# First norm of a decoder trunk: token tiles of chunk one loaded ahead of x's third chunk, squares after the scaling, first weights in two halves, another order of passes

## The chip, the core and the metric

The kernel runs on one core of one Trainium2 chip. The metric is the device time of one execution in microseconds (us), the median of several runs. TensorE is PE in the profile (its weight loads are PEld), VectorE is DVE, ScalarE is ACT, GpSimd is POOL and SyncE is SP. ACTq, SPq and POOLq are the engines' own instruction queues where they issue DMAs.

## The reference

Two layers over 16 meta tokens and 1024 tokens of width 1024. The change lies in the first norm and in the first input projections of layer 0.

```python
def rms_norm(x, gain):
    xf = x.astype(jnp.float32)
    y = xf * lax.rsqrt(jnp.mean(xf * xf, axis=-1, keepdims=True) + EPS)
    return (y * gain.astype(jnp.float32)).astype(x.dtype)

def conv_mixer(h, w_in, dw_kernel, dw_bias, ln_gain, ln_bias, w_out):
    proj = jnp.einsum("bld,dc->blc", h, w_in)
    u, g, z = jnp.split(proj, 3, axis=-1)
    v = u * jax.nn.sigmoid(g)
    # depthwise causal convolution of 31 taps over v, layer norm, SiLU,
    # times silu(z), projection with w_out
    ...

h = jnp.concatenate([meta, x], axis=1)          # 1040 tokens
for i in range(DEPTH):                          # layer 0: conv, layer 1: differential attention
    h = h + mixer_i(rms_norm(h, norm_gain[i]))
return rms_norm(h, final_norm_gain)[:, N_META:]
```

## The kernel before

Activations lie with the channels on the partitions: `x_t[k]` (k = 0 to 7) holds 128 channels by 1040 tokens. The tokens come in three chunks (`CH`) of 348, 346 and 346; numbers in names count from 0, so the first chunk is chunk 0. Weights come in strips of 128 output channels (`wf`, 512 KB). Each fp32 operand is split in two: a high part made by a copy on ACT (`wh` of the weights, `hh` of the activations) and a low part made by a subtraction (`wl`, `hl`; the function `lo_part`). `hh[k]` and `hl[k]` are the two halves of a tile that the profile calls hp. A projection of a strip on a chunk is 24 matmuls: 8 of wh with hh, 8 of wh with hl, 8 of wl with hh (`passes`, called by `project`).

The first norm runs in parts. The string `ORDER` sets in which order the code of these parts is written, each with its chunk number:

- u (`unscaled`): `hh` on ACT and `hl` on DVE are made from x times the gain, without the norm's scale, so that the strips g0 and u0 can be projected before the scale is known (p, `first_strips`). What is missing is multiplied into the result later (`sig0`, `vr0`).
- k (`load_tokens`): SP loads `chn` and `sub_g` and the nine tiles xk0 to xk8 (the last is called hsum), which hold 128 or 96 tokens on the partitions and their 1024 channels along the row. xk0 to xk2 are chunk 0, and so on.
- t (`statistics`): the sum of squares of each token, by a square with an accumulator on ACT (two tiles of a chunk) or a reduction on DVE (one tile); then the reciprocal root on a few numbers (`tk`); then diagonal matrices `dg` on DVE, which PE multiplies with ones (tile n0), so that the scale of each token stands on all partitions. ACT copies it to `n0_r`.
- s (`scaled`): DVE multiplies x by gain and scale in place, ACT copies it to `hh`, and DVE (k even) or POOL (k odd) makes `hl`. From these all other strips are projected, strip 1 (g1, u1) first.

After this the convolution stage runs strip by strip: ACT scales shifted copies (pr), POOL adds them (pb, L522), DVE does other taps (L535), PE projects the next strips (g, u, z).

The code's order is only the start: a scheduler orders each engine's instructions when the kernel is built, and each engine then runs its list strictly in that order. `tc.high_priority` moves instructions forward in it, `tc.issue_after(i)` puts one behind the instruction i. An SP DMA also waits for an earlier DMA whose semaphore it uses again, so that a limited number is under way. Weight strips have two buffers (`wf`); strips 0 and 1 of the list are g0 and u0, whose `wl` is made on POOL.

Of the kernel before, what the change touches and what calls it, by code (L numbers as in the profile page):

```python
# [15 lines left out]
ALU = mybir.AluOpType  # L16
# [46 lines left out]
DIR1 = True  # L63
WL = "GG"
SP_R = 2000
ORDER = "u0_p0_u1_p1_u2_k0_p2_t0_s0_t1_s1_t2_s2"
FC = [(512, 256), (768, 256)]
HXM = 6
WB = 2
# [23 lines left out]
def trunk(  # L93
# [63 lines left out]
    class Weights:  # L157
# [6 lines left out]
        def prepare(self):  # L164
            if self.done == len(self.order):
                return
            n = self.done
            src, eng = self.order[n]
            self.done += 1
            wf = gp.tile([P, KD, P], F32, tag="wf", name=f"wf{n}", bufs=2)  # L170
            SP.dma_start(out=wf, in_=src)
            keep = self.kept.get(n - len(self.order))
            if keep:
                wh, wl = keep()
            elif n in self.staged:
                wh, wl = stage(0, f"wh{n}", F32R), scratch[-1].tile([P, T], F32R, tag="vr", name=f"wl{n}", bufs=VR)
                wh, wl = [t[:, :D].rearrange("p (k c) -> p k c", c=P) for t in (wh, wl)]
            else:
                wh = gp.tile([P, KD, P], F32R, tag="wh", name=f"wh{n}", bufs=WB)
                wl = gp.tile([P, KD, P], F32R, tag="wl", name=f"wl{n}", bufs=WB)  # L180
            A.activation(out=wh, in_=wf, func=AF.Copy)  # L181
            lo_part(eng, wl, wf, wh.bitcast(F32))
            self.ready.append((wh, wl))

# [112 lines left out]
    with ExitStack() as st0:  # L297
# [40 lines left out]
        V.memset(tk, 1.0)  # L338
        x_sum = pair("n0")
        last_pair = pair("gu0")  # L340
        scale_of = {}

        def load(ci):
            c0, w = CH[ci]
# [4 lines left out]
        def statistics(ci):  # L349
# [5 lines left out]
            for b in range(9)[bs]:  # L355
                r0, n = TB[b]
                t = x_k[b][:n]
                if TKE.split("_")[ci][b % 3] == "A":
                    A.activation(out=t, in_=t, func=AF.Square, accum_out=tk[:n, 0, b : b + 1])
                else:  # L360
                    V.tensor_tensor_reduce(
                        out=t, in0=t, in1=t, scale=1.0, scalar=0.0, op0=ALU.mult, op1=ALU.add,
                        accum_out=tk[:n, 0, b : b + 1],
                    )
            with tc.high_priority(offset=SP_R):
                s, x, t, r = (tk[:, j, bs] for j in range(4))
                V.tensor_scalar(out=x, in0=s, scalar1=1.0 / D, scalar2=EPS, op0=ALU.mult, op1=ALU.add)
# [25 lines left out]
        def scaled(ci):  # L393
            c0, w = CH[ci]
            cs = slice(c0, c0 + w)
            for k in range(KD):
                t = x_t[k][:, cs]
                V.scalar_tensor_tensor(
                    out=t, in0=t, scalar=mod[:, k, 0:1], in1=scale_of[ci], op0=ALU.mult, op1=ALU.mult
                )  # L400
                A.activation(out=hh[k][:, cs], in_=t, func=AF.Copy)  # L401
                lo_part(V if k in LOV[ci] else G, hl[k][:, cs], t, hh[k][:, cs].bitcast(F32))

        def load_tokens(_):
            SP.dma_start(out=chn, in_=chan)
            SP.dma_start(out=sub_g, in_=subln)
            for (r0, n), t in zip(TB, x_k):
                SP.dma_start(out=t[:n], in_=xk[r0 : r0 + n])

        def first_strips(ci):  # L410
            for n, (kind, w_) in enumerate((("g", gw), ("u", uw))):
                o = last_pair[:, 512 * n : 512 * n + 512] if ci == 2 else mm(f"{kind}0_{ci}")
                (gates0, ups0)[n].extend(project(w_, hh, hl, lambda _: o, CH[ci : ci + 1]))

        gates0, ups0 = [], []
        SP.dma_start(out=mod, in_=model)
# [1 line left out]
        load(0)  # L418
        weights.prepare()
        load(1)  # L420
        load(2)
        gw, uw = weights.get(), weights.get()
        parts = {"u": unscaled, "p": first_strips, "t": statistics, "s": scaled, "k": load_tokens}
        for step in ORDER.split("_"):
            e = parts[step[0]](int(step[1]))
            if step == "t2":
# [885 lines left out]
```

## Time and profile before

| | us |
|---|---|
| median of 3 runs | 1464.42 (1463.52 to 1465.74) |
| the profiled execution, its own time | 1462.38 |
| its span, first to last instruction | 1460.6 |
| PE busy | 1411.1 (97%) |
| DVE busy | 1123.2 (77%) |
| ACT busy | 885.0 (61%) |
| POOL busy | 803.1 (55%) |

The shares are averages over stages. Up to about 73 us the first norm and strips 0 and 1 run; to about 530 us the convolution, in which POOL, DVE and PE are all nearly full; then the rest of layer 0 and the attention, in which PE is. A row of a timeline gives the start, the time from the first to the last of the instructions merged in it, what they are, and in brackets how long the engine was idle before and what ended that.

### The profile page before, as it was taken

How to read it: one execution, taken by the hardware profiler on the slowest of the kernel's cores; microseconds unless marked ns; L12 is line 12 of the kernel's file. 1: busy time of each engine (PE TensorE's matmuls, PEld its weight loads, DVE VectorE, ACT ScalarE, POOL GpSimd, SP SyncE). 2: the span in 40 equal slices, each digit the busy share in tenths (PEclk: the TensorE clock that was granted, in tenths of full speed). 3: DMA queues.
4: the chain of work that ended last, by engine and by line, in shares of the span. 5: the costliest groups of instructions: out<-in, count | busy, mean ns of one | idle time of the engine just before them, and what ended most of it. 6: DMA issues, size and time to landing. Idle time of an engine off the chain costs nothing.

```text
span 1460.6 us, 24069 instructions
## 1 busy us (share of the span) xinstructions
PE 1411.1 (97%) x8798; PEld 1323.8 (91%) x8798; DVE 1123.2 (77%) x2121; ACT 885.0 (61%) x1604; POOL 803.1 (55%) x640
## 2 busy tenths in 40 slices
PE   8899999999999999899999999999999999999997
PEld 7799999999999999899998878988889899897786
DVE  5999999999999998988545311578788687786774
ACT  5765655565556668766224411668778777786652
POOL 1599999999999940044014501525345354353572
PEclk9999999999999999999999999999999999999999
DMA  9121112112111232654544634223221322338532
GB/s 300 31 73 44 59 53 64 45 44 66 66 44 44 92 116 97 192 167 153 169 158 132 200 99 124 64 70 104 85 81 63 114 81 77 104 89 296 171 124 94
DMA packets 81128, 155.15 MB, mean 106 GB/s; under 512 B 7121, under 2 KB 46546, under 8 KB 79986
## 3 DMA queue, kind: packets, MB, share of 16 engines
q1 hardware_dynamic: 67906, 131.01, 28.8%
q0 software_dynamic: 3824, 13.37, 2.9%
q10 hardware_dynamic: 9280, 9.23, 1.9%
q8 instruction: 69, 1.13, 0.3%
q14 instruction: 49, 0.40, 0.1%
HBM read 111.06 MB, written 34.01 MB: 99 GB/s over the span
## 4 chain that ended last, share of the span: by engine, by line
PE 51%; POOL 16%; DVE 13%; ACT 7%; issue 7%; DMA 5%; SPq 1%; POOLq 0%; DVEq 0%; ACTq 0%
POOL pb L522 15%; PE c L199 8%; PE v L199 6%; PE q L199 5%; PE k L199 5%; PE za L199 5%; PE z L199 4%; PE ao L199 3%; PE o L199 3%; ACT pr L521 2%; PE s L1000 2%; PE s L1001 2%; PE u L199 2%; PE tp L1034 2%; DVE wl L155 2%
## 5 line engine op out<-in xcount | busy, mean ns | idle before, releaser
L522 POOL TENSOR_TENSOR pb<-pr,pb 128x521 f32<-128x521 f32 (+1 forms) x272 | 386.6, 1430 | 14.7
L521 ACT ACTIVATE pr<-vr,chn 128x521 f32<-128x521 f32 x224 | 150.6, 724 | 129.7 <-POOL pb L522 129.5
L199 PE MATMUL c<-b,wh 128*128 128x260 f32 x1024 | 186.3, 284 | 3.7 <-ACT sz L447 1.6
L535 DVE SCALAR_TENSOR_TENSOR ev<-vr,chn,ev 128x520 f32<-128x520 f32 x240 | 181.1, 754 | 1.2
L181 ACT ACTIVATE wh<-wf 128x1024 fp32r<-128x1024 f32 x115 | 121.0, 1052 | 96.2 <-PE c L199 54.2
L199 PE MATMUL g<-hp,wh 128*128 128x346 f32 (+1 forms) x752 | 154.6, 329 | 13.5 <-ACT hp L401 5.3
L199 PEld LDWEIGHTS c<-b,wh 128*128 128x128 f32 x1024 | 158.8, 189 | 4.6 <-ACT sz L447 1.9
L199 PE MATMUL u<-hp,wh 128*128 128x346 f32 (+1 forms) x752 | 158.0, 323 | 2.3 <-ACT wh L181 2.2
L155 DVE TENSOR_TENSOR wl<-wf,wh 128x1024 fp32r<-128x1024 f32 x81 | 128.7, 1591 | 39.8 <-ACT wh L181 39.1
L199 PE MATMUL c<-b,wl 128*128 128x260 f32 x512 | 144.4, 284 | 3.5 <-DVE wl L155 3.5
L199 PEld LDWEIGHTS g<-hp,wh 128*128 128x128 f32 x752 | 126.8, 191 | 18.2 <-ACT hp L401 5.5
L155 POOL TENSOR_TENSOR wl<-wf,wh 128x1024 fp32r<-128x1024 f32 x34 | 84.7, 2490 | 97.8 <-ACT wh L181 54.1
L199 PE MATMUL z<-hp,wh 128*128 128x346 f32 (+1 forms) x768 | 134.9, 321 | 0.8 <-ACT sig L479 0.8
L535 DVE SCALAR_TENSOR_TENSOR od<-xs,wc,od 128x520 f32<-128x520 f32 x176 | 132.5, 753 | 0.0
L199 PEld LDWEIGHTS u<-hp,wh 128*128 128x128 f32 x752 | 126.8, 189 | 3.2 <-ACT wh L181 3.2
L707 POOL TENSOR_TENSOR total<-hsq,total 128x520 f32<-128x520 f32 x12 | 20.5, 1710 | 194.4 <-DMA wf<-conv_out 98.1
L199 PEld LDWEIGHTS z<-hp,wh 128*128 128x128 f32 x768 | 124.1, 188 | 1.2 <-ACT sig L479 1.1
L1008 ACT ACTIVATE p<-p,st 128x272 f32<-128x272 f32 (+7 forms) x128 | 100.5, 785 | 39.8 <-DVE st L1003 39.3
L199 PEld LDWEIGHTS c<-b,wl 128*128 128x128 f32 x512 | 97.1, 190 | 4.1 <-DVE wl L155 4.0
L199 PE MATMUL g<-hp,wl 128*128 128x346 f32 (+1 forms) x376 | 83.6, 321 | 0.0
L199 PE MATMUL v<-wv,g 128*128 128x512 f32 x352 | 83.5, 394 | 0.0
L1000 PE MATMUL s<-k,q 128*128 128x256 f32 (+6 forms) x224 | 77.0, 348 | 5.3 <-DVE st L1003 5.3
(298 smaller groups left out, 3433.2 us busy)
## 6 DMA issues: line engine op xcount, KB each, us to landing
wf<-conv_in SPq DMA_DIRECT2D x48, 512.0 KB, 3.6
wf<-conv_out SPq DMA_DIRECT2D x32, 512.0 KB, 3.9
wf<-attn_in SPq DMA_DIRECT2D x32, 512.0 KB, 3.7
wf<-attn_out SPq DMA_DIRECT2D x17, 512.0 KB, 3.6
sz_d<-sz ACTq DMA_DIRECT2D x32, 260.0 KB, 3.7
szr<-sz_d SPq DMA_DIRECT2D x16, 520.0 KB, 4.5
v<-v_d POOLq DMA_DIRECT2D x8, 1024.0 KB, 5.3
ya_d<-yb SPq DMA_DIRECT2D x28, 256.0 KB, 2.5
```

What stands on the lines that cost most here:

```text
L155: return eng.tensor_tensor(out=out_, in0=full, in1=hi, op=ALU.subtract)
L181: A.activation(out=wh, in_=wf, func=AF.Copy)
L199: PE.matmul(o, a[k], b[k], start=start and i == 0, stop=stop and i == tot - 1)
L521: A.activation(out=d, in_=src, func=AF.Copy, scale=w)
L522: G.tensor_tensor(out=dst, in0=d, in1=dst, op=ALU.add)
L535: V.scalar_tensor_tensor(out=dst, in0=src, scalar=w, in1=dst, op0=ALU.mult, op1=ALU.add)
L707: (V if SQA[m] == "V" else G).tensor_tensor(out=total[:, ns], in0=sq, in1=total[:, ns], op=ALU.add)
L1000: PE.matmul(o[:, :wm], q2[m][:, qs], k2[m][:, c0 : c0 + wm], start=True, stop=False)
L1001: PE.matmul(o[:, :wm], q2[m][:, qs], kl2[m][:, c0 : c0 + wm], start=False, stop=True)
L1008: A.activation(out=p[:, :n], in_=p[:, :n], func=AF.Exp, scale=-1.0, bias=least, accum_out=st[:, 1:2],)
L1034: PE.transpose(tp[:, (kb - kb0) * P : (kb - kb0 + 1) * P], p0[:, kb * P : (kb + 1) * P], ident)
```

## The change

- `load_tokens` gets a chunk number and loads three tiles. xk0 to xk2 are issued ahead of x's chunk 2, xk3 to xk5 behind weight strips 2 and 3, then `chn` and `sub_g`, then xk6 to xk8.
- `ORDER` puts t0 ahead of u2 and p2, and s0 ahead of t1.
- In `statistics` the squares on ACT are put behind the last copy of `scaled` issued so far, the reductions on DVE behind the last multiplication of it.
- Weight strip 0 comes in two DMAs of 256 KB, one from SP and one from ACT, and its high part in two copies.
- `first_strips` writes the matmuls itself: for g0 on chunk 0 the hl matmuls follow two behind the hh ones; for all others the order is hh, wl, hl.

```diff
-ORDER = "u0_p0_u1_p1_u2_k0_p2_t0_s0_t1_s1_t2_s2"
+ORDER = "u0_p0_u1_p1_t0_u2_p2_s0_t1_s1_t2_s2"
...
             wf = gp.tile([P, KD, P], F32, tag="wf", name=f"wf{n}", bufs=2)
-            SP.dma_start(out=wf, in_=src)
+            if n:
+                SP.dma_start(out=wf, in_=src)
+            else:
+                for q, ks in ((SP, slice(0, KD // 2)), (A, slice(KD // 2, KD))):
+                    q.dma_start(out=wf[:, ks], in_=src[:, ks])
...
-            A.activation(out=wh, in_=wf, func=AF.Copy)
+            for ks in (slice(0, KD),) if n else (slice(0, KD // 2), slice(KD // 2, KD)):
+                A.activation(out=wh[:, ks], in_=wf[:, ks], func=AF.Copy)
...
-        scale_of = {}
+        scale_of, scaled_by, gained_by = {}, [], []
...
-                    A.activation(out=t, in_=t, func=AF.Square, accum_out=tk[:n, 0, b : b + 1])
+                    with tc.issue_after(scaled_by[-1]) if scaled_by else ExitStack():
+                        A.activation(out=t, in_=t, func=AF.Square, accum_out=tk[:n, 0, b : b + 1])
                 else:
-                    V.tensor_tensor_reduce(
+                    with tc.issue_after(gained_by[-1]) if gained_by else ExitStack():
+                        V.tensor_tensor_reduce(
...
-                V.scalar_tensor_tensor(
+                e = V.scalar_tensor_tensor(
                     out=t, in0=t, scalar=mod[:, k, 0:1], in1=scale_of[ci], op0=ALU.mult, op1=ALU.mult
                 )
-                A.activation(out=hh[k][:, cs], in_=t, func=AF.Copy)
+                gained_by.append(e.ins)
+                scaled_by.append(A.activation(out=hh[k][:, cs], in_=t, func=AF.Copy).ins)
...
-        def load_tokens(_):
-            SP.dma_start(out=chn, in_=chan)
-            SP.dma_start(out=sub_g, in_=subln)
-            for (r0, n), t in zip(TB, x_k):
+        def load_tokens(ci):
+            for (r0, n), t in list(zip(TB, x_k))[3 * ci : 3 * ci + 3]:
...
-                (gates0, ups0)[n].extend(project(w_, hh, hl, lambda _: o, CH[ci : ci + 1]))
+                c0, w = CH[ci]
+                cs = slice(c0, c0 + w)
+                wh, wl = w_
+                ab = [[(wh, hh, k) for k in range(KD)], [(wh, hl, k) for k in range(KD)], [(wl, hh, k) for k in range(KD)]]
+                if ci == 0 and n == 0:
+
+                    ab = [j for two in zip_longest(ab[0], [None] * 2 + ab[1]) for j in two if j] + ab[2]
+                else:
+                    ab = ab[0] + ab[2] + ab[1]
+                for j, (a, x, k) in enumerate(ab):
+                    PE.matmul(o[:, :w], a[:, k], x[k][:, cs], start=j == 0, stop=j == 3 * KD - 1)
+                (gates0, ups0)[n].append((c0, w, o[:, :w]))
...
         load(1)
+        load_tokens(0)
         load(2)
         gw, uw = weights.get(), weights.get()
-        parts = {"u": unscaled, "p": first_strips, "t": statistics, "s": scaled, "k": load_tokens}
+        load_tokens(1)
+        SP.dma_start(out=chn, in_=chan)
+        SP.dma_start(out=sub_g, in_=subln)
+        load_tokens(2)
+        parts = {"u": unscaled, "p": first_strips, "t": statistics, "s": scaled}
```

What the scheduler makes of it, at three places. The first is PE's list where the scale of chunk 1 (n0 from dg1) is spread over the partitions, during strip 1 on chunk 0 (g1_0 and u1_0 with weights 2 and 3); before:

```order
L199 MATMUL g1_0_621<-hp6_101,wh2_165 128x348
L199 MATMUL u1_0_646<-hp6_101,wh3_611 128x348
L376 MATMUL n0_124<-dg1_426,ones_63 128x128 x2
L199 MATMUL g1_0_621<-hp7_102,wh2_165 128x348
L199 MATMUL u1_0_646<-hp7_102,wh3_611 128x348
L376 MATMUL n0_124<-dg1_426,ones_63 128x96
L199 MATMUL g1_0_621<-hp0_95,wh2_165 128x348
```

and after:

```order
L204 MATMUL u1_0_648<-hp5_100,wl3_614 128x348
L204 MATMUL u1_0_648<-hp6_101,wl3_614 128x348
L204 MATMUL u1_0_648<-hp7_102,wl3_614 128x348
L383 MATMUL n0_124<-dg1_428,ones_63 128x128 x2
L383 MATMUL n0_124<-dg1_428,ones_63 128x96
L204 MATMUL g1_1_676<-hp0_95,wh2_170 128x346
L204 MATMUL u1_1_701<-hp0_95,wh3_613 128x346
```

The scale of chunk 1 stood after 14 of the 48 matmuls of strip 1 on chunk 0 and now stands behind all 48; that of chunk 2 (n0 from dg2), in the same way, after 12 of strip 1 on chunk 1 before and behind all 48 now, and that of chunk 0 behind all of chunk 2 of strips 0 before, and in the midst of it now.

The second is DVE's list around the scaling of chunk 0 (x0 to x7 times n0); before:

```order
L375 TENSOR_SCALAR dg0_385<-ident_65,tk_122 96x96
L361 ISA xk7_121,tk_122<-xk7_121 128x1024
L361 ISA tk_122 128x1
L155 TENSOR_TENSOR wl3_612<-wf3_609,wh3_611 128x1024
L233 TENSOR_TENSOR tk_122<-tk_122 128x3
L367 TENSOR_SCALAR tk_122<-tk_122 128x3
L234 SCALAR_TENSOR_TENSOR tk_122<-tk_122 128x3
L483 TENSOR_TENSOR sig0_506<-g0_0_185,n0_r_112 128x348
L485 TENSOR_TENSOR vr0_504<-u0_0_210,n0_r_112 128x348
L235 SCALAR_TENSOR_TENSOR tk_122<-tk_122 128x3
L398 SCALAR_TENSOR_TENSOR x0_87<-x0_87,mod_76,n0_124 128x348
```

and after, from the end of that scaling:

```order
L405 SCALAR_TENSOR_TENSOR x7_94<-x7_94,mod_76,n0_124 128x348
L368 ISA xk4_118,tk_122<-xk4_118 128x1024
L368 ISA tk_122 128x1
L155 TENSOR_TENSOR wl2_171<-wf2_168,wh2_170 128x1024
L476 TENSOR_SCALAR chn_86<-chn_86 128x16x31
L841 TENSOR_SCALAR sub_s_8266<-sub_g_77 128x1
L155 TENSOR_TENSOR hp0_95<-x0_87,hp0_95 128x348
L155 TENSOR_TENSOR hp2_97<-x2_89,hp2_97 128x348
L155 TENSOR_TENSOR hp4_99<-x4_91,hp4_99 128x348
L155 TENSOR_TENSOR wl3_614<-wf3_611,wh3_613 128x1024
L155 TENSOR_TENSOR hp6_101<-x6_93,hp6_101 128x348
```

The reductions of xk4 and xk7 and the low parts of weights 2 and 3 stood ahead of chunk 0's scaling; now xk4, both low parts and the work on `chn` stand behind it, between the scaling and chunk 0's hl, and xk7 in the same way behind chunk 1's scaling.

The third is ACT's list at the start, its DMAs and the copies of the first weight strip (wh0) and of chunk 0; before:

```order
L347 DMA x1_88<-xt 128x348
L347 DMA x3_90<-xt 128x348
L347 DMA x5_92<-xt 128x348
L181 ACTIVATE wh0_129<-wf0_127 128x1024
L347 DMA x7_94<-xt 128x348
L387 ACTIVATE hp0_95<-x0_87,mod_76 128x348
```

and after:

```order
L175 DMA wf0_127<-conv_in 128x512
L352 DMA x1_88<-xt 128x348
L352 DMA x3_90<-xt 128x348
L186 ACTIVATE wh0_130<-wf0_127 128x512 x2
L352 DMA x5_92<-xt 128x348
L352 DMA x7_94<-xt 128x348
L394 ACTIVATE hp0_95<-x0_87,mod_76 128x348
```

The second half of the weights goes out ahead of x1 and x3, and the DMA of x5 moves behind the copies that wait for these weights.

## Rows read from the trace of the kernel before

**Rows 1.** The page's part 4, shares of the chain that ended last.

```profile
PE 51%; POOL 16%; DVE 13%; ACT 7%; issue 7%; DMA 5%; SPq 1%; POOLq 0%; DVEq 0%; ACTq 0%
```

**Rows 2.** Stretches: length; busy us (instructions) by engine, PEclk, DMA share, GB/s.

```profile
0.00:17.10 17.10, 12.26 (x45) 9.95 (x46) 10.56 (x20) 13.03 (x24) 5.57 (x8) 1.00 0.91 311
...
40.00:47.00 7.00, 3.65 (x13) 3.65 (x14) 6.74 (x18) 6.26 (x15) 3.24 (x4) 0.52 0.22 75
...
73.00:530.00 457.00, 449.48 (x2819) 446.56 (x2818) 439.44 (x618) 272.48 (x421) 440.33 (x299) 1.00 0.19 60
530.00:580.00 50.00, 50.00 (x310) 49.49 (x309) 41.29 (x62) 34.78 (x53) 0.00 (x0) 1.00 0.30 92
```

**Rows 3.** Timeline of PE, first 75 us: start, us, what [idle before].

```profile
6.89 5.74 PE L199 MATMUL g<-hp,wh 128*128 128x348 f32 x14 [1.74 <-ACT hp L387]
14.31 0.92 PE L199 MATMUL g<-hp,wh 128*128 128x348 f32 x2 [1.67 <-DVE hp L388]
15.06 1.42 PE L199 MATMUL g<-hp,wl 128*128 128x348 f32 x8
...
34.09 1.44 PE L199 MATMUL gu<-hp,wl 128*128 128x346 f32 x8
...
43.35 0.66 PE L199 MATMUL g<-hp,wh 128*128 128x348 f32 x1 [5.31 <-ACT hp L401]
...
55.63 0.81 PE L376 MATMUL n<-dg,ones 128*128 128x128 f32 x6
...
69.67 1.44 PE L199 MATMUL u<-hp,wl 128*128 128x346 f32 x8
```

**Rows 4.** Timeline of POOL, first 75 us.

```profile
6.45 2.37 POOL L155 TENSOR_TENSOR wl<-wf,wh 128x1024 fp32r<-128x1024 f32 x1 [5.13 <-ACT wh L181]
11.36 2.51 POOL L155 TENSOR_TENSOR wl<-wf,wh 128x1024 fp32r<-128x1024 f32 x1 [2.55 <-ACT wh L181]
43.76 3.61 POOL L155 TENSOR_TENSOR hp<-x,hp 128x348 fp32r<-128x348 f32 x4 [29.89 <-ACT hp L401]
...
67.19 8.41 POOL L522 TENSOR_TENSOR pb<-pr,pb 128x521 f32<-128x521 f32 x5
```

**Rows 5.** Timeline of DVE around the two POOL operations of the start.

```profile
6.87 2.32 DVE L388 SCALAR_TENSOR_TENSOR hp<-x,mod,hp 128x348 fp32r<-128x348 f32 x1 [5.72 <-ACT hp L387]
...
11.57 2.68 DVE L388 SCALAR_TENSOR_TENSOR hp<-x,mod,hp 128x348 fp32r<-128x348 f32 x1
```

**Rows 6.** Timeline of DVE, 33 to 63 us.

```profile
33.56 1.22 DVE L361 CUSTOM_DVE_ANT_0 xk<-xk 128x1024 f32<-128x1024 f32 x1
...
34.78 1.22 DVE L155 TENSOR_TENSOR wl<-wf,wh 128x1024 fp32r<-128x1024 f32 x1
...
40.81 0.52 DVE L483 TENSOR_TENSOR sig<-g,n_r 128x348 f32<-128x348 f32 x1
...
48.48 1.37 DVE L155 TENSOR_TENSOR hp<-x,hp 128x348 fp32r<-128x348 f32 x3
...
51.46 3.96 DVE L398 SCALAR_TENSOR_TENSOR x<-x,mod,n 128x346 f32<-128x346 f32 x8
...
59.65 2.99 DVE L398 SCALAR_TENSOR_TENSOR x<-x,mod,n 128x346 f32<-128x346 f32 x6
```

**Rows 7.** Timeline of ACT, first 75 us.

```profile
5.31 1.06 ACT L181 ACTIVATE wh<-wf 128x1024 fp32r<-128x1024 f32 x1 [3.28 <-DMA wf<-conv_in]
...
6.27 3.91 ACT L387 ACTIVATE hp<-x,mod 128x348 fp32r<-128x348 f32 x8
...
56.48 0.46 ACT L378 ACTIVATE n_r<-n 128x346 f32<-128x346 f32 x1 [0.53 <-PE n L376]
...
65.81 2.58 ACT L521 ACTIVATE pr<-vr,chn 128x521 f32<-128x521 f32 x4
```

**Rows 8.** SP's own queue at the start: start, us of the issue.

```profile
1.20 0.43 SPq L171 DMA_DIRECT2D wf<-conv_in  x1
```

**Rows 9.** The page's part 6: DMA issues, KB each, us to landing.

```profile
ya_d<-yb SPq DMA_DIRECT2D x28, 256.0 KB, 2.5
```

More of the change, by code (lines that the diff above doesn't have):

```diff
@@ L358, in statistics @@
                 if TKE.split("_")[ci][b % 3] == "A":
-                    A.activation(out=t, in_=t, func=AF.Square, accum_out=tk[:n, 0, b : b + 1])
-                else:
-                    V.tensor_tensor_reduce(
-                        out=t, in0=t, in1=t, scale=1.0, scalar=0.0, op0=ALU.mult, op1=ALU.add,
-                        accum_out=tk[:n, 0, b : b + 1],
-                    )
+                    with tc.issue_after(scaled_by[-1]) if scaled_by else ExitStack():
+                        A.activation(out=t, in_=t, func=AF.Square, accum_out=tk[:n, 0, b : b + 1])
+                else:
+                    with tc.issue_after(gained_by[-1]) if gained_by else ExitStack():
+                        V.tensor_tensor_reduce(
+                            out=t, in0=t, in1=t, scale=1.0, scalar=0.0, op0=ALU.mult, op1=ALU.add,
+                            accum_out=tk[:n, 0, b : b + 1],
+                        )
             with tc.high_priority(offset=SP_R):
```

## The prediction

> **What bounds the kernel now.** I read first the chain that ended last: more than half of it is PE, then POOL and DVE [rows 1]. Then the stretches: from 73 to 530 us PE works 449.5 of 457 us, POOL 440.3 and DVE 439.4, and from 530 to 580 us PE works all of the time [rows 2]. So after the start three engines are full together: what the start saves stays saved if PE, POOL and DVE all get it, and what one of them loses is lost. The start itself is read from the timelines. PE waits 1.74 us for its first hh and 1.67 us for the last hl but one of chunk 0 [rows 3], then runs 128 matmuls from 15.06 to 35.53 us, 0.16 us each, and then has little to do until 43.35 us, with 5.31 us idle at the end, because the scaled chunk 0 is not there [rows 3]. DVE scales chunk 1 from 51.46 and chunk 2 from 59.65 us [rows 6], PE ends strip 1 at 71.1 us [rows 3], and POOL begins to add taps at 67.19 us [rows 4]. These last three are the marks at which the new start must be early.
>
> **The first weights.** The strip is issued at 1.20 us and its copy on ACT starts at 5.31 [rows 8, 7]. A DMA of 256 KB elsewhere lands in 2.5 us [rows 9], so the halves land between 3.7 us and no earlier than now; I take 4.2, since they and three x tiles share the engines: 1.1 us gained, bounds 0 and 1.6. The Trainium skill, "DMA: Bandwidth & Descriptors", section "Issuing engines are not separate DMA queues", says that DMAs of different issuing engines run on the same 16 DMA engines and that several issuers save only the time of issuing. By that the halves would be worth one issue, 0.4 us, and the forecast below would be 0.7 us later. No run here shows the halves yet.
>
> **Chunk 0 up to its last hl.** ACT then copies the weights until about 5.25, POOL starts wl0 at 5.35 and holds DVE's first hl until 8.05: before, POOL's operation ran from 6.45 to 8.82 and DVE's, started at 6.87, ended at 9.19 [rows 4, 5]. Seven more at 0.49 each (0.49 from the eight of 3.96 us [rows 6]) would put the start of the eighth at 10.95. ACT needs 3.91 us for its eight copies [rows 7] and 1.06 for the next weights, so POOL's wl1 starts at 10.3, or up to 0.5 us later if the x tiles whose DMA moved behind the copies, or the weights, are late. That is ahead of the eighth hl, which is held as one was before: started at 11.57, ended at 14.25, POOL from 11.36 for 2.51 us [rows 4, 5]. With POOL from 10.6 the last hl ends near 13.5, against 14.7 before: 1.2 us early.
>
> **Loading xk0 to xk2 earlier.** By 17.1 us the DMAs have moved 311 GB/s, 5.3 MB [rows 2]; that is the first two strips (1.0 MB), two chunks of x (2.8 MB) and these three tiles (1.4 MB). So they land at about 17 to 18 us. x's chunk 2 comes about 4 us later, near 22, and is needed by PE only at 26.5 (below): nothing is lost. The sums of squares of xk0 to xk2 and the few small steps behind them are ready by 25.
>
> **Scale of chunk 0.** In PE's new list 97 matmuls stand between the last hl of chunk 0 and the last two that spread this scale; 97 at 0.16 from 13.65, with the first of the three, is 29.4. From such matmuls to the first scaled tile it takes 0.85 us to ACT's copy (55.63 to 56.48), 0.46 for it, and about 0.45 each for the multiplications of g0 and u0 (0.52 with the start-up): 2.2 us, here 2.1 as one of the three is done [rows 3, 7, 6]. The scaling starts at 31.5; before, PE's first matmul with its result was at 43.35 [rows 3]. So about 10 us are won here, and the question is what is kept.
>
> **Strip 1 on chunk 0.** The scaling takes 3.9 us (35.4). Behind it DVE now has xk4 (1.22), wl2 (1.22) and 0.45 us of work on the taps before the first hl (0.43) [rows 6]: 38.7. These have two operands in SBUF, and POOL makes its four hl of 0.9 us each just then [rows 4]; each may hold DVE up, 0 to 1.4 us in all. I take 1.2, since POOL held the operations of rows 5 for its whole length: 40.0. Two hl, wl3 and the fourth hl follow (0.86, 1.14 and 0.43): 42.4. PE has ended strips 0 at 35.0 and the 16 hh matmuls at 37.6, so it idles 2.4 us, and after the fourth hl it still has 20 matmuls: 45.7.
>
> **Scale of chunks 1 and 2.** Both stand behind all 48 matmuls of the strip in PE's new list, though dg1 is ready at about 44. Chunk 1's scaling starts at 45.7 + 2.2 = 47.9, 3.6 us earlier than before (51.46). Then scaling 3.9, POOL's hold 0 to 0.9 (I take 0.5), xk7 1.22, first hl 0.43: 54.0. From here PE has 32 matmuls, 5.1 us: 59.1. Chunk 2's scaling starts at 59.1 + 2.2 = 61.3, while it was 59.65 [rows 6]. The 10 us have gone: before, DVE alone set the pace and the scales were spread in the middle of a strip; now DVE waits for PE behind each strip, and PE for DVE's hl. What follows is the same work in nearly the same order, so PE ends strip 1 near 72.8 instead of 71.1, and POOL starts at about 68.8, after ACT's first copies of 2.58 us for four [rows 7]: **1.6 us later**. The bounds: no hold by POOL and the best DMA time give 59.0 for chunk 2, full holds and no gain from the halves 63.3; so 0.7 us gained to 3.7 lost.
>
> **The other edits.** Putting wl ahead of hl lets PE run where hl is late; in strips 0 DVE's hl of chunks 1 and 2 are ahead of PE anyway, so it is worth nothing there. The interleaved hl of g0 saves the six hl matmuls that before ran behind hh, which lay in the wait for DVE: nothing. `chn` comes about 10 us later than before and is first needed at 39: nothing. SP's queue has as many DMAs as before, ACT's one more, issued while ACT has no work; the next strip's DMA waits for wl2 as before and is needed after 70 us: nothing.
>
> **Sum.** 1462.38 for the profiled execution + 1.6 = 1464.0; the median of the runs is 2.0 above the profiled one, so 1466.0, bounds 1463.7 to 1468.1.
>
> **Rivals.** (1) *The eighth hl gets ahead of wl1.* Its start (10.95) and that of wl1 (10.3 to 10.8, later if the moved x tiles land later) are close. If DVE starts first, the last hl ends at 11.45, and then dg0, ready at 24.5, holds PE's list instead: 2.0 us less, 1464.0. The Trainium skill, "SBUF — State Buffer", section "Who interferes with whom", has it that a DVE instruction with two SBUF inputs and a GpSimd one that reads SBUF exclude each other, and that the one issued first blocks the other fully. The two holds of rows 4 and 5, where POOL was first both times, agree with it; by that rule this rival hangs on which of the two starts first. Against it: 0.2 us or more are missing.
> (2) *The convolution is dealt better.* PE idles 7.5 us between 73 and 530 us [rows 2], and the scheduler has ordered this stretch anew on PE, ACT and DVE. If half of this idle time goes, or the waits between DVE and PE in strip 1 turn out half as long, some 5 us are gained on the forecast: 1461.0. For it: the new list has the work for the next strips ahead; against: POOL is 96% busy there (440.3 of 457), and its list has hardly changed.
> (3) *PE's clock falls in strip 1.* After the idle time up to 43.35 the granted clock was 0.52 over 40 to 47 us, the lower of the two levels (1.2 GHz), while two shorter waits within the first 17 us left it at 1.00 [rows 3, 2]. In the new list PE waits about 2 us for chunk 1's scaling, then works two matmuls per 0.49 us, then waits 1.7 us. If the clock falls there, 32 matmuls on the way to chunk 2's scale take 0.28 us (13 in 3.65 us of work over 40 to 47 [rows 2]) instead of 0.16: 3.8 us later, 1469.8, slower. It decides if PE is idle as long as before 43.35; the waits counted here are each half of that, which speaks against it.
> (4) *The start is as early as it is meant to be*, all three marks 4 us early, because DVE's work behind each scaling finds no hold and PE reaches the scales earlier than counted: 1460.4. It needs both other ends at once.
>
> **Numbers.** Forecast 0.45, rival 1 0.2, rival 2 0.13, rival 3 0.12, rival 4 0.1. A measurement of this kernel can tell 0.2%, 2.9 us, from no change. Faster by more: rivals 2 and 4 but for a small part, with a little of rival 1, 0.23. Slower by more: rival 3 and a third of the forecast's own range, 0.26. Within: 0.51. The predicted time is 1466.0. The range reaches into rivals 2 and 3: 1460.6 to 1469.6.
>
> **What would show it.** The weights' first copy at 4.2 us; the last hl of chunk 0 behind POOL's wl1; chunk 0's scaling at 31.5, chunk 1's at 47.9, chunk 2's at 61.3; PE's waits of 2 us ahead of the first hl of strip 1 and ahead of chunk 1; POOL's first tap near 68.8. If chunk 2's scaling starts before 58, the loop between PE and DVE is shorter than I say; if the marks are as forecast and the time is not, the cause is the convolution's new order.

## The result and the profile after

The kernel after takes 1473.22 us (median of 7 runs, 1469.20 to 1479.60) against 1464.06 beside it: ratio 1.0057, 95% interval 1.0044 to 1.0071. It is 8 to 9 us slower; 1466.0 was forecast, with a range that ended at 1469.6. The profiled execution took 1477.28 us, with a span of 1475.5. It is the second longest of its seven, and that of the kernel before (1462.38) is shorter than any of the seven beside it, so the two spans differ by more than the medians do.

The start, from the timeline of ACT (start, us, what, in brackets the idle time before and what ended it); it answers [rows 7]:

```profile
5.01 0.63 ACT L186 ACTIVATE wh<-wf 128x512 fp32r<-128x512 f32 x1 [2.98 <-DMA wf<-conv_in]
5.55 0.61 ACT L186 ACTIVATE wh<-wf 128x512 fp32r<-128x512 f32 x1
...
12.38 1.06 ACT L186 ACTIVATE wh<-wf 128x1024 fp32r<-128x1024 f32 x1 [1.64 <-DMA wf<-conv_in]
18.19 1.06 ACT L365 ACTIVATE xk<-xk 128x1024 f32<-128x1024 f32 x1 [0.94 <-DMA xk<-xk]
...
21.87 1.06 ACT L365 ACTIVATE xk<-xk 96x1024 f32<-96x1024 f32 x1 [2.52 <-DMA xk<-xk]
```

POOL, same columns, answering [rows 4]:

```profile
6.24 2.35 POOL L155 TENSOR_TENSOR wl<-wf,wh 128x1024 fp32r<-128x1024 f32 x1 [4.93 <-ACT wh L186]
13.52 2.40 POOL L155 TENSOR_TENSOR wl<-wf,wh 128x1024 fp32r<-128x1024 f32 x1 [4.93 <-ACT wh L186]
...
72.84 27.05 POOL L544 TENSOR_TENSOR pb<-pr,pb 128x521 f32<-128x521 f32 x18 [1.84 <-ACT pr L543]
```

DVE, answering [rows 5, 6]:

```profile
7.45 4.97 DVE L395 SCALAR_TENSOR_TENSOR hp<-x,mod,hp 128x348 fp32r<-128x348 f32 x8 [6.29 <-DMA x<-xt]
13.95 5.79 DVE L395 SCALAR_TENSOR_TENSOR hp<-x,mod,hp 128x346 fp32r<-128x346 f32 x8 [1.54 <-ACT hp L394]
...
38.42 1.73 DVE L368 CUSTOM_DVE_ANT_0 xk<-xk 128x1024 f32<-128x1024 f32 x1
40.09 2.01 DVE L155 TENSOR_TENSOR wl<-wf,wh 128x1024 fp32r<-128x1024 f32 x1
...
46.93 0.66 DVE L382 TENSOR_SCALAR dg<-ident,tk 128x128 f32<-128x128 f32 x3
50.94 3.97 DVE L405 SCALAR_TENSOR_TENSOR x<-x,mod,n 128x346 f32<-128x346 f32 x8
...
60.16 0.66 DVE L382 TENSOR_SCALAR dg<-ident,tk 128x128 f32<-128x128 f32 x3
65.09 2.99 DVE L405 SCALAR_TENSOR_TENSOR x<-x,mod,n 128x346 f32<-128x346 f32 x6
```

PE, answering [rows 3]:

```profile
7.46 5.43 PE L429 MATMUL g<-hp,wh 128*128 128x348 f32 x16 [2.34 <-ACT hp L394]
...
27.99 0.49 PE L383 MATMUL n<-dg,ones 128*128 128x128 f32 x2 [2.43 <-DVE dg L382]
...
42.97 0.59 PE L204 MATMUL g<-hp,wh 128*128 128x348 f32 x2 [1.83 <-DVE hp L155]
...
48.68 0.80 PE L383 MATMUL n<-dg,ones 128*128 128x128 f32 x6
52.08 0.42 PE L204 MATMUL g<-hp,wh 128*128 128x346 f32 x1 [2.60 <-ACT hp L409]
57.75 0.58 PE L204 MATMUL g<-hp,wh 128*128 128x346 f32 x2 [1.14 <-DVE hp L155]
...
62.90 0.80 PE L383 MATMUL n<-dg,ones 128*128 128x128 f32 x6
66.23 2.59 PE L204 MATMUL g<-hp,wh 128*128 128x346 f32 x5 [2.53 <-ACT hp L409]
...
76.39 1.44 PE L204 MATMUL u<-hp,wl 128*128 128x346 f32 x8
```

Read these together. dg1 stands on DVE at 47.6 us and PE reaches it at 48.68; dg2 stands at 60.8 and PE reaches it at 62.90, each time behind the whole strip: 1.1 and 2.1 us late. Then PE waits 2.60 and 2.53 us for the scaling that this scale releases, and in strip 1 on chunks 0 and 1 it waits 1.83 and 1.14 us for the first hl. That is the loop between PE and DVE of the prediction. POOL's first tap comes at 72.84 us; it was at 67.19 [rows 4].

Stretches of the same trace: length; busy us (instructions) of PE, PEld, DVE, ACT, POOL; PE's granted clock; DMA share; GB/s. The third and fourth answer [rows 2]:

```profile
52.00:56.00 4.00, 3.92 (x14) 3.62 (x15) 4.00 (x7) 4.00 (x9) 3.28 (x4) 0.59 0.01 4
66.00:73.00 7.00, 6.77 (x20) 5.57 (x21) 7.00 (x16) 5.17 (x11) 3.86 (x5) 0.53 0.00 0
73.00:530.00 457.00, 448.32 (x2806) 446.32 (x2805) 430.33 (x615) 275.05 (x424) 441.76 (x298) 1.00 0.18 58
530.00:580.00 50.00, 50.00 (x310) 49.42 (x309) 38.62 (x57) 30.31 (x46) 5.32 (x5) 1.00 0.32 103
```

So 5.65 us are lost by POOL's first tap, of 14.9 us between the two spans. The rest comes later: the first `mean_ps` on PE, which ends the convolution, comes at 537.66 us, 8.4 us later than the 529.25 of the kernel before (its row stands below).

### The profile page after: what moved, and what is told of

Read it like the earlier page. It is cut to its first block, busy times and chain, and to the rows that moved or that the text cites. A ratio compares the mean times of both kernels' runs of the same rounds, so it can differ in the third digit from the quotient of the medians.

```text
span 1475.5 us, 24073 instructions
## 1 busy us (share of the span) xinstructions
PE 1422.1 (96%) x8798; PEld 1333.7 (90%) x8798; DVE 1115.3 (76%) x2121; ACT 886.9 (60%) x1605; POOL 803.0 (54%) x640
## 4 chain that ended last, share of the span: by engine, by line
PE 54%; POOL 17%; DVE 9%; ACT 8%; issue 7%; DMA 5%; SPq 0%; POOLq 0%; DVEq 0%; ACTq 0%
POOL pb L544 16%; PE c L204 8%; PE v L204 6%; PE z L204 6%; PE q L204 5%; PE za L204 5%; PE k L204 5%; PE ao L204 4%; PE o L204 3%; ACT pr L543 2%; PE u L204 2%; PE s L1022 2%; PE s L1023 2%; PE tp L1056 2%; PE g L204 2%
## 5 line engine op out<-in xcount | busy, mean ns | idle before, releaser
L186 ACT ACTIVATE wh<-wf 128x1024 fp32r<-128x1024 f32 (+1 forms) x116 | 121.3, 1046 | 107.5 <-PE c L204 51.9
L204 PE MATMUL g<-hp,wh 128*128 128x348 f32 (+1 forms) x720 | 147.2, 327 | 13.2 <-ACT hp L409 5.1
L204 PE MATMUL u<-hp,wh 128*128 128x348 f32 (+1 forms) x720 | 153.3, 325 | 2.2 <-ACT wh L186 2.2
L155 DVE TENSOR_TENSOR wl<-wf,wh 128x1024 fp32r<-128x1024 f32 x81 | 122.9, 1518 | 38.2 <-ACT wh L186 32.2
L204 PEld LDWEIGHTS g<-hp,wh 128*128 128x128 f32 x720 | 121.0, 191 | 17.0 <-ACT hp L409 6.5
L729 POOL TENSOR_TENSOR total<-hsq,total 128x520 f32<-128x520 f32 x12 | 20.6, 1713 | 199.0 <-DMA xr<-xn 100.1
L204 PEld LDWEIGHTS u<-hp,wh 128*128 128x128 f32 x720 | 122.7, 191 | 3.2 <-ACT wh L186 3.1
L204 PE MATMUL g<-hp,wl 128*128 128x348 f32 (+1 forms) x360 | 80.9, 321 | 0.0
```

Source lines behind the costliest of these rows:

```text
L155: return eng.tensor_tensor(out=out_, in0=full, in1=hi, op=ALU.subtract)
L186: A.activation(out=wh[:, ks], in_=wf[:, ks], func=AF.Copy)
L204: PE.matmul(o, a[k], b[k], start=start and i == 0, stop=stop and i == tot - 1)
L729: (V if SQA[m] == "V" else G).tensor_tensor(out=total[:, ns], in0=sq, in1=total[:, ns], op=ALU.add)
```

## The experiments

Theory A: the two rules that put the squares behind the scaling are the cause; through them the scales of chunks 1 and 2 come behind the whole strip, and PE and DVE take turns. The rival: DMAs that land later cost the time at the start. Others were formed on the way. The new order of the passes was not run alone; a_noafter has it, with all of the change but the rules. The results together; "scaling" is the start of DVE's scaling of chunks 0, 1 and 2, "first tap" that of POOL's adding, "to mean_ps" the time from there to the first mean_ps on PE, the last three columns from one trace each:

| kernel | median us | before, beside it | ratio (95%) | scaling 0, 1, 2 | first tap | to mean_ps |
|---|---|---|---|---|---|---|
| before | | | 1 | 41.7, 51.5, 59.7 | 67.2 | 462.1 |
| after | 1473.22 | 1464.06 | 1.0057 (1.0044 to 1.0071) | 34.5, 50.9, 65.1 | 72.8 | 464.8 |
| after_again | 1472.84 | 1466.24 | 1.0047 (1.0034 to 1.0060) | 31.3, 47.6, 61.7 | 69.5 | 464.4 |
| a_noafter | 1465.94 | 1466.24 | 0.9998 (0.9988 to 1.0007) | 32.4, 51.5, 59.7 | 67.2 | 462.4 |
| b_follow | 1475.52 | 1466.24 | 1.0066 (1.0048 to 1.0084) | 38.5, 56.3, 70.5 | 78.2 | 461.8 |
| a_t0late | 1469.88 | 1466.24 | 1.0031 (1.0018 to 1.0043) | 31.1, 48.8, 63.0 | 70.8 | 461.9 |
| a_onlydve | 1470.88 | 1465.33 | 1.0042 (1.0027 to 1.0056) | 33.0, 50.1, 64.2 | 72.0 | 463.2 |
| a_onlyact | 1468.62 | 1465.33 | 1.0024 (1.0006 to 1.0041) | 32.1, 49.7, 62.6 | 70.3 | 463.0 |
| a_pin | 1468.93 | 1465.33 | 1.0033 (1.0021 to 1.0046) | 31.6, 46.8, 59.0 | 66.0 | 463.6 |
| a_pin_again | 1469.51 | 1466.20 | 1.0032 (1.0017 to 1.0048) | 33.5, 48.6, 60.8 | 67.8 | 463.9 |
| n_pin | 1462.70 | 1465.33 | 0.9993 (0.9981 to 1.0006) | 34.1, 49.9, 58.1 | 65.7 | 461.9 |
| n_pin_again | 1464.22 | 1466.20 | 0.9988 (0.9976 to 1.0000) | 34.4, 50.3, 58.5 | 66.0 | 462.4 |
| b_load | 1465.73 | 1466.20 | 1.0001 (0.9988 to 1.0014) | 34.5, 52.3, 60.5 | 68.0 | 462.3 |
| b_halves | 1468.67 | 1466.20 | 1.0014 (0.9999 to 1.0029) | 43.4, 53.1, 61.3 | 68.8 | 462.4 |

### The rules, off and alone

**after_again** is the kernel after once more.

> The changed kernel once more, to see how far its time and its start spread. All theories: chunk 2's scaling starts near 65.1 us as in the profile after (59.65 before), strip 1 ends near 77.8. Theory A (the squares behind the scaling make PE and DVE take turns) and rival B (the weights and token tiles land later than counted) put the loss in the start, so the runs should spread little about +7 to +9 us. Rival C (the clock falls by chance later, between 470 and 1400 us) expects runs 1468 to 1480 again, each with its own falls.

**a_noafter** is the kernel after without the rules.

```diff
-                    with tc.issue_after(scaled_by[-1]) if scaled_by else ExitStack():
+                    with ExitStack():
                         A.activation(out=t, in_=t, func=AF.Square, accum_out=tk[:n, 0, b : b + 1])
...
-                    with tc.issue_after(gained_by[-1]) if gained_by else ExitStack():
+                    with ExitStack():
```

> The changed kernel without the two issue_after around the squares and reductions. In PE's list the scale of chunk 2 moves from behind all 48 matmuls of strip 1 on chunk 1 to behind its first 12; that of chunk 1 stays behind strip 1 on chunk 0. Theory A: one of the two turns goes, chunk 2's scaling starts 3 us or more earlier than 65.1, and the time falls by 3 to 5 us, to about 1469. Rival B: nothing changes (within 1 us).

**b_follow** is the kernel before with the rules alone (the `+` lines of `issue_after`, `gained_by` and `scaled_by` of the change, nothing else).

> The kernel before with nothing but the two issue_after around the squares and reductions; its loads, weights and order of passes are those of before. Theory A: PE's list now has the scales of chunks 1 and 2 behind all of strip 1 on chunks 0 and 1, so the turns of about 16 and 14 us appear here too: chunk 0's scaling starts at 36, chunk 2's near 66 instead of 59.65, and the kernel is 5 to 7 us slower than before. Rival B: its DMAs are those of before, so it stays within 2 us of before.

The rules alone cost 9 us, where 5 to 7 were expected, and without them nothing is left of the loss: 1465.94 against 1466.24, where 3 to 5 us were expected back. In b_follow the first tap comes 11.0 us later than in the kernel before, and from there to mean_ps it takes no longer (461.8). Both scalings of a_noafter that follow chunk 0's start where they did in the kernel before [rows 6], though chunk 0's starts 9.3 us earlier. DVE of a_noafter:

```profile
32.42 3.98 DVE L405 SCALAR_TENSOR_TENSOR x<-x,mod,n 128x348 f32<-128x348 f32 x8
...
45.20 0.65 DVE L382 TENSOR_SCALAR dg<-ident,tk 128x128 f32<-128x128 f32 x3
...
46.15 0.66 DVE L382 TENSOR_SCALAR dg<-ident,tk 128x128 f32<-128x128 f32 x3
...
51.47 3.97 DVE L405 SCALAR_TENSOR_TENSOR x<-x,mod,n 128x346 f32<-128x346 f32 x8
...
59.68 2.99 DVE L405 SCALAR_TENSOR_TENSOR x<-x,mod,n 128x346 f32<-128x346 f32 x6
```

The first dg row is dg1, the second dg2. Here dg2 is ready by 46.8 us, ahead of strip 1 on chunk 1, because the squares of chunk 2 wait for no scaling; PE spreads it early in that strip (55.49 us), as before. In the kernel after dg2 isn't there until 60.8.

The repeat of the kernel after shows what the DMAs do, which is scatter. DVE of after_again:

```profile
31.25 3.98 DVE L405 SCALAR_TENSOR_TENSOR x<-x,mod,n 128x348 f32<-128x348 f32 x8
...
47.59 3.96 DVE L405 SCALAR_TENSOR_TENSOR x<-x,mod,n 128x346 f32<-128x346 f32 x8
...
61.74 2.99 DVE L405 SCALAR_TENSOR_TENSOR x<-x,mod,n 128x346 f32<-128x346 f32 x6
```

The same program starts chunk 0's scaling 3.3 us earlier than in the first trace, since the last tile of chunk 0's tokens was squared at 19.75 us and not at 21.87 and PE didn't wait for dg0. The steps between the scalings stay: 16.41 and 16.34 us, then 14.15 in both. Chunk 2's scaling came at 61.74, not at the 65.1 that the expectation had. The two profiled executions differ by 2.7 us in span (1475.5 and 1472.8), about what the first tap differs by, so the start does count; but with the tokens early the kernel is still 6.6 us slower than before in that round. a_noafter has the same loads and no loss, so late DMAs are not the cause.

### Which rule, and where t0 stands

**a_onlydve** keeps the rule on DVE's reduction alone, **a_onlyact** that on ACT's squares alone; in each the other `with` line is replaced as in a_noafter.

> The kernel after with the rule kept for the one reduction on DVE alone; the two squares on ACT are free. PE's list has dg1 and dg2 in the same places as the kernel after (197th and 247th, behind the whole strip). Theory A: the places decide, so scalings 31 to 35, 47.5 to 51 and 61.5 to 65, and the time 1471 to 1474, as the kernel after. Theory D (it is ACT's squares behind its eight copies that delay the scale, the work and not the place): chunk 2's scaling at 59.7 to 60.5 and the time at 1466 to 1468.

> The kernel after with the rule kept for the two squares on ACT alone; the reduction on DVE is free. PE's list has dg1 and dg2 in the same places as the kernel after. Theory A: as the kernel after, 1471 to 1474, chunk 2's scaling at 61 to 65 us, less about 0.5 since xk4 may be reduced before the scaling. Theory E (it is the 1.7 us reduction on DVE between the scaling and the first hl that costs the time): chunk 0's hl start 1.7 us earlier, chunk 2's scaling at 58 to 60 and the time at 1466 to 1468.

Either rule is enough to put dg1 and dg2 behind the whole strip; with DVE's alone PE spreads them at 47.80 and 62.02 us. Both kernels are slower than before. Theories D and E forecast 1466 to 1468 for one of them. With DVE's rule alone neither came. With ACT's rule alone the time, 1468.62, is nearer to E, and the trace is A's: chunk 2 starts at 62.55, where A had it, and not at 58 to 60. So it is enough that some of a chunk's squares wait for the scaling of the chunk before, on either engine; the size of the loss is not settled by these two, since the rest of the kernel is ordered otherwise too (below).

**a_t0late** is the kernel after with t0 behind p2.

```diff
-ORDER = "u0_p0_u1_p1_t0_u2_p2_s0_t1_s1_t2_s2"
+ORDER = "u0_p0_u1_p1_u2_p2_t0_s0_t1_s1_t2_s2"
```

> The changed kernel with the statistics of chunk 0 written behind chunk 2 of strips 0, so that PE's list has all three matmuls that spread chunk 0's scale behind 17 of chunk 2's matmuls and does not wait for dg0 ahead of them. In the profile after PE waited 2.43 us there and then ran 3.2 us at the lower clock. All theories: this wait goes, chunk 0's scaling starts at 30.5 to 32 instead of 34.5. Theory A: the turns of 16.4 and 14.1 us behind it stay, so chunk 2's scaling starts at 61 to 62.5 and the time falls by 2.5 to 4 us. Rival C: the time does not follow the start.

PE's wait for dg0 is gone and chunk 0's scaling starts at 31.11. The loop is there too (48.8 and 63.0), and the kernel loses 3.6 us at the first tap as in the time. Theory A's forecast for the time came (3.0 us below the kernel after), but not for its reason: the step to chunk 1 grew to 17.7 us, the first tap lies between those of the two traces of the kernel after, and what is gained lies behind it (461.9 to mean_ps against 464.4 and 464.8).

### The place of the scale, and what is left

**a_pin** is the kernel after with the scale of the next chunk pinned ahead of wl's matmuls in strip 1 (`spread` holds the last matmul of each n0; `project` hands it on as `pin` for strip 1 alone, in lines not shown).

```diff
-        for a, b in ((wh, mh), (wh, ml), (wl, mh)):
-            for k in range(n):
-                PE.matmul(o, a[k], b[k], start=start and i == 0, stop=stop and i == tot - 1)
-                i += 1
+        for j, (a, b) in enumerate(((wh, mh), (wh, ml), (wl, mh))):
+            with tc.issue_after(pin) if pin is not None and j == 2 else ExitStack():
+                for k in range(n):
+                    PE.matmul(o, a[k], b[k], start=start and i == 0, stop=stop and i == tot - 1)
+                    i += 1
...
-                    PE.matmul(acc[:, o : o + n], ones[:n], dg[:n], start=True, stop=True)
+                    last_mm = PE.matmul(acc[:, o : o + n], ones[:n], dg[:n], start=True, stop=True)
+                spread.append(last_mm.ins)
```

> The kernel after, with one thing added: in strip 1 the matmuls of wl with hh are put behind the matmuls that spread the scale of the next chunk, so that PE reaches dg1 after 32 of the 48 matmuls of strip 1 on chunk 0 (181st in its list, before 197th), and dg2 after 32 of those on chunk 1. Theory A (the place of the scales behind the whole strip is what makes PE and DVE take turns): chunk 1's scaling starts about 1.1 us earlier against chunk 0's than in the kernel after, since dg1 is ready at about 44.3 when chunk 0's scaling starts at 31.3 and PE reached it at 45.4; chunk 2's about 3 us earlier in all; the end of PE's strip 1 and POOL's first tap 2 to 3 us earlier, and the time 2 to 4 us below the kernel after, 1469 to 1471. Theory C (DVE's own list sets the pace: reduction, low parts of weights and hl behind each scaling, and the place on PE hides nothing): no scaling moves by more than 0.5 us and the time stays at 1472 to 1474.

The place is worth what A said: against chunk 0's scaling, chunk 2's starts 27.4 us later (59.04 - 31.64) instead of 30.5, as in a_noafter (27.3), and POOL's first tap is 1.2 us earlier than in the kernel before. And yet the kernel is slower than before, by 3 to 7 us. So the start is not the whole loss. **a_pin_again** is the same kernel.

> The kernel named a_pin once more. Its start was as early as that of the kernel before (POOL's first tap 65.99 us against 67.19), and yet its time was 3.6 us above. Theory F (the two rules change the order of the whole convolution on PE, DVE and ACT, and this order is worse): from POOL's first tap to the first mean_ps on PE 463 to 465 us again (462.0 before), PE's wait ahead of mean_ps about 3 us again (1.5 before), and the time 3 to 5 us above the kernel before. Theory G (chance of that round: PE's clock and DMAs late in the kernel): 462 us, and the time within 1.5 us of the kernel before.

Again the first tap stands near that of the kernel before (67.75 against 67.19), and the time is 3.3 us above. The expectation calls the wait ahead of mean_ps PE's; it is DVE that waits for mean_ps, 3.2 us in both traces of a_pin, 2.8 in both of the kernel after, 1.5 in the ten others. The rules move much more than the start: without them POOL's list is that of the kernel before throughout and DVE's from its 78th instruction on, while with one or both of them the lists of PE, DVE and ACT are in another order until early in the output projection (tile c), and POOL's at a few places of the convolution; only from there on are they the same again. The signs of theory F came (463.9 us to mean_ps, a wait of 3.2, a time 3.3 above), but in general it goes too far: b_follow and a_t0late have both rules and another order too, and take 461.8 and 461.9 us to mean_ps. What the new order costs depends on how it falls out. Where the convolution ends in the kernel after, DVE, then PE:

```profile
535.51 0.70 DVE L560 TENSOR_TENSOR v<-ev,pb 128x520 f32<-128x520 f32 x1 [0.79 <-POOL pb L548]
...
540.93 1.31 DVE L617 TENSOR_SCALAR mean<-mean_ps 128x520 f32<-128x520 f32 x2 [2.79 <-PE mean_ps L580]
```

```profile
535.12 2.71 PE L204 MATMUL z<-hp,wh 128*128 128x348 f32 x16
537.66 1.04 PE L580 MATMUL mean_ps<-hsum,ones 128*128 128x260 f32 x4
```

And in the kernel before, PE:

```profile
528.22 0.64 PE L199 MATMUL z<-hp,wl 128*128 128x348 f32 x3
529.25 1.14 PE L558 MATMUL mean_ps<-hsum,ones 128*128 128x260 f32 x4 [0.39 <-DVE v L538]
```

In the kernel before PE is waiting when the tile v is ready. After, v is ready at 536.2 us, but PE has 16 matmuls of z ahead of mean_ps in its list: 1.5 us, the same kind of loss as in strip 1. From the end of POOL's last operation of the convolution to the first mean_ps it takes 2.2 us in both traces of the kernel after, 1.6 and 1.5 in a_pin, and 0.8 in the ten others. Another 1.4 us lies on POOL, which works without a pause of more than 0.15 us from 67.19 to 528.46 us before (461.3) and from 72.84 to 535.48 after (462.6): the operations are the same in number, and what differs is which of them take about 1 us longer than others of their kind. Those on hsum take 2.4 us or 3.4 to 3.6; three of 14 are long before and four after, which is 1.0 of the 1.4 us; one is in b_follow, five are in a_pin. What they meet on DVE is a subtraction wl; a long and a short one in the kernel after:

```profile
337.08 3.56 POOL L564 TENSOR_TENSOR hsum<-v,hsum 128x1040 f32<-128x1040 f32 x1
337.12 1.21 DVE L155 TENSOR_TENSOR wl<-wf,wh 128x1024 fp32r<-128x1024 f32 x1
```

```profile
190.64 2.46 POOL L564 TENSOR_TENSOR hsum<-v,hsum 128x1040 f32<-128x1040 f32 x1
192.19 1.98 DVE L155 TENSOR_TENSOR wl<-wf,wh 128x1024 fp32r<-128x1024 f32 x1
```

In all 14 traces each long one has a wl that began before it, or at most 0.05 us behind its start, and ended 1.1 to 1.3 us in. A wl that began later in one left it at 2.4 us and was itself held until 1.0 to 2.4 us after its end.

Behind mean_ps the trace can be cut by tiles: c is the output projection of the convolution, s the attention's scores. Durations in us, one trace each, for c and s from the first to the last start of a matmul; the first column holds the six traces whose convolution has the order of before:

| stretch | before, a_noafter, n_pin (2), b_load, b_halves | after (2) | a_pin (2) | the four others with a rule |
|---|---|---|---|---|
| first tap to mean_ps | 461.9 to 462.4 | 464.4, 464.8 | 463.6, 463.9 | 461.8 to 463.2 |
| mean_ps to c | 58.6 | 58.9, 59.0 | 57.3 | 59.7 |
| c | 195.5 to 199.0 | 198.4, 198.6 | 202.1, 204.9 | 194.9 to 197.4 |
| s | 449.5 to 452.2 | 453.4, 453.7 | 452.3, 454.1 | 450.5 to 454.4 |

Taking means, the kernel after stands 4.0 us later at the first tap (71.2 against 67.15), loses 2.4 to mean_ps, 0.4 to c, 0.8 in c and 2.9 in s; the two spans average 1474.2, the six 1463.8. Why s is longer stays open: the lists are the same there. Two things differ in s between traces of one kernel and of several: PE's wait for the DMA of kl (0.6 to 3.5 us in the six, 1.7 and 3.7 after), and short falls of the granted clock at changing places, which cost the stretch's length times one minus its granted clock (1.7 to 3.4 us in the six, 5.1 and 1.7 after). The two together are 6.1 us after and 3.6 in the six on the mean, 2.5 of the 2.9; less both, s takes 446.6 to 448.0 us in 13 of the 14 traces (444.4 in a_t0late). Seven of the eight traces with a rule have an s of 452.3 us or more, and the six without have 452.2 or less, so the loss goes with the rules in these traces; no experiment shows how.

For a_pin the same cut shows that theory F's stretch is the smaller part. On the mean of its two traces it loses 1.5 us to mean_ps, gains 1.2 from there to c, and loses 5.8 in c, where PE waits 10.5 and 12.6 us against 6.3 to 9.1 in the six, and 2.5 in s. What makes PE wait longer in c is not shown.

### The other parts, and a better version

**b_load** is the kernel before with the new order of the loads (`load_tokens` by chunk, at its new places) and with k0 left out of `ORDER`; nothing else of the change.

> The kernel before with the new order of loading alone (xk0 to xk2 ahead of x's chunk 2, xk3 to xk5 behind weight strips 2 and 3, chn and sub_g behind them). PE's list has the scale of chunk 0 in the midst of strips 0 and that of chunk 1 behind strip 1 on chunk 0. If the loading alone brings the scale forward: xk2 lands at 18 to 22 us, chunk 0's scaling starts at 31 to 35 us instead of 41.7, chunk 1's and chunk 2's at 49 to 52 and 59 to 60, since DVE's work decides there, and the time is within 2 us of the kernel before. If what the start gains were kept: chunk 2's at 53 to 56 and the time 4 us lower.

Chunk 0's scaling starts 7.3 us earlier than before, chunk 2's 0.8 later, and the time is the same. The gain is spent in strip 1, where DVE's work and the place of the scale on PE (50.04 us) decide.

**b_halves** is the kernel before with the two half DMAs and two copies.

> The kernel before with the first weight strip in two halves alone. By the prediction's term the first copy on ACT starts at 4.2 us; by the trace of the kernel after (first copy at 5.01 us, against 5.31 of a whole strip before) it starts at 4.9 to 5.1. The order of the convolution is unchanged, and the time is within 1.5 us of the kernel before either way.

The first copy starts at 5.18 us, against 5.31 [rows 7]: 0.13 us, less than expected. The order of all that follows is that of the kernel before; in its one trace chunk 0's tokens are late, the scalings come 1.6 us later, and the time is 2.5 us above and not within 1.5, with an interval that just reaches 1. So the halves are not shown to gain or to lose.

**n_pin** is a_noafter with the pin of a_pin.

> The kernel after without the two rules that put the squares behind the scaling, and with the same pin as the kernel named a_pin, which moves dg1 from the 197th to the 181st place of PE's list; dg2 stays at the 211th. Theory A: without the rules chunk 1's scaling started at 51.47 us because PE came to dg1 at 49.21 while DVE had it ready at 46.8; with the pin it starts at 48.5 to 49.2, chunk 2's at 56.6 to 57.5 (59.68 without), POOL's first tap at 64 to 65 (67.2), and the time is 2 to 3 us below the kernel without the rules, 1463 to 1464, just below the kernel before. Theory C: chunk 2's scaling, which DVE reaches without idle time, stays at 59.7, and the time at 1466.

> The kernel named n_pin once more: without the two rules, with the scale of chunk 1 pinned ahead of wl's matmuls in strip 1. POOL's first tap at 64.5 to 65.7, from there 462 us to mean_ps since the order of the convolution is that of the kernel before, and the time 1 to 3 us below the kernel before. If the first result was chance: no difference.

The scale of chunk 1 now meets DVE without an idle gap. (The 46.8 of the expectation is dg2's; dg1 stood at 45.85 in a_noafter, and DVE idled 3.10 us ahead of chunk 1.) PE of n_pin, then DVE, where the first dg row is dg1:

```profile
47.52 0.80 PE L385 MATMUL n<-dg,ones 128*128 128x128 f32 x6
```

```profile
46.83 0.65 DVE L384 TENSOR_SCALAR dg<-ident,tk 128x128 f32<-128x128 f32 x3
...
47.78 0.66 DVE L384 TENSOR_SCALAR dg<-ident,tk 128x128 f32<-128x128 f32 x3
48.55 0.52 DVE L519 SCALAR_TENSOR_TENSOR vr<-sig,vr 128x348 f32<-128x348 f32 x1
48.99 0.51 DVE L508 TENSOR_TENSOR sig<-g,n_r 128x346 f32<-128x346 f32 x1
49.42 0.57 DVE L510 TENSOR_TENSOR vr<-u,n_r 128x172 f32<-128x172 f32 x2
49.91 3.97 DVE L408 SCALAR_TENSOR_TENSOR x<-x,mod,n 128x346 f32<-128x346 f32 x8
```

It gains 1.2 to 1.5 us at chunk 2 and the first tap, somewhat less than theory A expected, while theory C's 59.7 did not come (58.1 and 58.5). Its median is 2.6 and 2.0 us below that of before in two rounds, with ratios of 0.9993 and 0.9988 whose intervals reach 1: about 0.1%, and not shown to be a gain. It has the lowest median of the kernels here, some 9 us under the kernel after.

## Why the prediction was wrong

**First weights, missed.** Forecast 4.2 us, measured 5.01 and, alone, 5.18; over all runs 4.90 to 5.18 with the halves and 5.31 to 5.41 without, so 0.1 to 0.5 us won, not 1.1. The 2.5 us of [rows 9] is a median over a kernel whose DMAs move 106 GB/s on the mean, and didn't hold at the start, where they move 311 [rows 2]. The other price that the prediction weighed, one issue of 0.4 us, lies within what was won. That agrees with the Trainium skill, "DMA: Bandwidth & Descriptors", section "Issuing engines are not separate DMA queues", by which several issuers save only the time of issuing.

**Last hl of chunk 0: rival 1 happened, without its gain.** The hl ended at 12.4 us, since wl1 on POOL started at 13.52 and not at 10.3: its weights landed only at 12.38. The hold fell on chunk 1's first hl instead. That rival's 2.0 us did not come: PE waited for dg0 until 27.99, since the tokens were late, and in after_again, where it didn't wait, it came to this scale only at 26.37. Its granted clock at the start was lower there than before: 0.53 over 8 to 15 us (0.57 over 8 to 12 in the first trace), against 1.00 [rows 2].

**Landing of xk0 to xk2, missed in size.** Forecast 17 to 18 us, measured 19.75 and 21.87 for the last tile. Counting bytes gave the earliest end. The step "dg0 ready at 25, PE at 26.5" had too little slack: PE waited 2.43 us in one trace and not at all in the other. Chunk 0's scaling was forecast for 31.5: 34.53 and 31.25.

**The loop in strip 1, right.** Forecast from chunk 0's scaling to chunk 1's 16.4 us, measured 16.41 and 16.34; to chunk 2's 13.4, measured 14.15 twice. PE's idle time on chunk 0 was forecast as 2.4; by the waits of the trace (0.26, 1.83 and 0.25) it is 2.3. Rival 3 happened in part. The granted clock was 0.59 from 52 to 56 us and 0.53 from 66 to 73, while it had stayed at 1.00 in the kernel before; the waits ahead of it, 2.60 and 2.53 us, were half of the 5.31 of [rows 3], which the prediction counted against this rival. It cost far less than the 3.8 forecast: on chunk 1 PE, though slow, still had to wait 1.14 us for the first hl, so the fall there cost nothing; on chunk 2 it takes 12.7 us from the scaling to PE's last matmul of strip 1 (65.09 to 77.8), and 11.4 before (59.65 to 71.1), but the first tap follows the scaling after 7.75 and 7.54 us, 0.2 apart. POOL's first tap was forecast for 68.8, measured 69.50 and 72.84.

**The sum, and this is the step that failed most.** The prediction has it that behind the scaling "what follows is the same work in nearly the same order", and took the new order of the convolution only as a rival that gains (1461.0). In the kernel after it cost 2.4 us by mean_ps, and 4 us more were lost behind that, most of them in s, where the way to the change stays open. In after_again the three scalings stood within 0.5 us of the forecast and the first tap 0.7 behind it, and the kernel was still 6.6 us slower than before in its round, where 1.6 was forecast. The prediction's own test, that with the marks as forecast and the time not the cause is the new order of the convolution, named a part of it; the range did not reach there, because this rival had only one sign. In the other trace the late tokens add to it: its first tap, at 72.84 us, is 4.0 behind the forecast.

## What to carry to other kernels

Where a scheduler orders the program, a rule put on a few instructions is a change of every list behind them: compare the lists far past the edit, and give a reordered stretch a loss as well as a gain. The same two rules cost the convolution 2.4 us in one kernel and nothing in another (b_follow). An earlier start is worth what the next shared engine gets: bringing chunk 0's scaling forward by 7 to 10 us was worth nothing while DVE's work and the place of the next scale in PE's list set the pace. When two engines hand work back and forth, look at where the handed-over instruction stands in the receiver's list before looking at its duration.

## What the hardware showed unexpectedly

Two executions of one program had the last of the same three 0.4 to 0.5 MB tiles ready for ACT at 19.75 and 21.87 us, 2 to 4 us behind the forecast from the bytes. PE's granted clock fell to the lower of its two levels (1.2 GHz, 0.53) behind a wait of 2.53 us with short gaps after it; in a_noafter it stayed at 1.00 over 52 to 60 us behind a wait of 2.60. POOL's operation on hsum takes 2.4 us, or 3.4 to 3.6 when a subtraction wl on DVE is ahead of it. And splitting the first 512 KB between two issuing engines brought it 0.1 to 0.5 us, though a 256 KB transfer elsewhere lands in 2.5 us [rows 9].
